# S5 phasor tables in half chunks with their own fragment, on a stream of their own in the first gate and up phase

## The chip, the core and the metric

The program runs on one core of a Trainium2 chip. TensorE (PE, with its weight loads PEld), VectorE (DVE), ScalarE (ACT) and GpSimd (POOL) each work through a list of instructions in order; SyncE (SP) holds the list of DMA issues, also in order. They wait for one another through semaphores. The metric is device time in microseconds of one launch.

## What is computed

Two layers of a streaming encoder on a sequence of 1024 positions and 1024 channels, float32. Layer 0 is forgetting attention followed by a SwiGLU; layer 1 is an S5 state-space mixer followed by another SwiGLU:

```python
def swiglu(h, w_gate, w_up, w_down):
    return (jax.nn.silu(h @ w_gate) * (h @ w_up)) @ w_down

def s5_mixer(h, w_in, log_dt, lam_re, lam_im, b_re, b_im, c_re, c_im, d_skip, w_glu, w_out):
    u = (h @ w_in).astype(f32)
    dt = jnp.exp(log_dt.astype(f32))[:, None]
    mag = jnp.exp(lam_re * dt)
    a_re = mag * jnp.cos(lam_im * dt)
    a_im = mag * jnp.sin(lam_im * dt)
    ...
    # x[k] = a * x[k-1] + (B u)[k] (complex, 64 groups of 64 states); y = Re(C x) + d * u
    y = jax.nn.gelu(y).astype(h.dtype)
    y = y * jax.nn.sigmoid(y @ w_glu)
    return y @ w_out
```

What S5 needs of its parameters alone (powers of `a`, products of these with `B` and `C`, and the phasors `e1 * e2`) does not depend on the data. The kernel makes these tables during the gate and up projections of layer 0, stores them in DRAM, and reads them back in the S5 mixer.

## The kernel before

**Gate and up.** `gate_up` (line 784) multiplies in 11 **pairs** p = 0..10 (one tile of gate with one of up, each with its partner half a matrix away). A pair is 14 **steps** s = 0..13 of 12 matmuls; each matmul is a product of high and low parts, and Strassen-like sums of weight quarters make 7 products do the work of 8. For each pair the weights are loaded as four 512 KB pages (`raw`, SP), summed on DVE (L819, L820, L825, L826), rounded to a high part on ACT (L807) and turned into a low part on DVE (L808). DVE and ACT also take the products out of PSUM (L871 to L888) and build the results `g_d` that SP stores (L898 to L906). The same function runs twice: in layer 0 (pairs from 762 to 1244 us of the trace) with the tables beside it, and in layer 1 (1810 to 2234 us) with nothing beside it.

**The tables beside it.** After the matmuls and the copies of a step, `gate_up` calls `next(beside)` if `when(p, s)` says so (L920). `beside` is the generator `s5_params` (L1129), and the set of steps is `(5, 9, 12)` in the pairs 2 to 9. After a start in pairs 0 to 2 it goes through 8 chunks, and each takes three calls:

1. *cp*: eight POOL products (L1183, L1184, L1187) into page `s5w0`, with `s5w1` as scratch. This is issued at step 12.
2. Step 5 of the next pair: the store of cp (L1197), 16 short matmuls on PE (L1201, **K matmuls**), two ACT copies and a POOL addition for `KT` (L1204, L1206, in `s5w1`), its store, then *bp*: six POOL products (L1237, L1238, L1239), again in `s5w0` with scratch `s5w1`.
3. Step 9: eight PE transposes of bp (L1168, **T transposes**), an ACT copy `T` into `s5w1` (L1170) and its store, then the **phasors** (`s5_rot`, L1217): six DVE products of 128x512 (L1237 to L1239, the helper `prod`), into `s5w0` with scratch `s5w1`. The phasors' store (L1228) is issued at the start of the next call, step 12, right ahead of the next chunk's cp.

So one chunk goes cp, K matmuls, KT, bp, T transposes, T, phasors and back to cp, always through the same two pages (28 and 32), each with one buffer: each stage waits until the stage before it has been read or stored.

**What sets the order.** The tile framework places the instructions of each engine in a fixed list when the kernel is built (nearly the program's order, with some moved by a priority), and adds the waits. `tc.issue_after(self.sp.ins)` keeps a store behind the latest weight load in SP's list. At run time every engine goes through its list in order.

**Names.** K matmuls and T transposes are also PE work: 16 and 8 short instructions for each chunk. `R1`, `R2`: the two factors of the phasors. `pw`: powers of `a`, read by cp and bp. `M`: a matrix of the mixer, whose first buffer lies in R1's page 30.

Of the kernel before, what the change touches and what calls it, by code (L numbers as in the profile page):

```python
# [20 lines left out]
NF = FF // P  # L21
# [137 lines left out]
class Trunk:  # L159
# [365 lines left out]
    def attend(self, c, o):  # L525
# [36 lines left out]
        def sums(hp):  # L562

            p2, r, x = self.pb(PTB, (P, P))[0:16], self.small("ri", (16, P)), self.R("RI")
            nc.tensor.transpose(p2, rs.pop(hp).rearrange("p a b -> p (a b)"), self.ident)
            nc.vector.reciprocal(r, p2)
            nc.sync.dma_start(self.ri_d[hp], r)
            for i in range(2):
                nc.sync.dma_start(x[i * 64:i * 64 + 64], self.bcast(self.ri_d[hp][i * 8:i * 8 + 8], D, 64))
            ri[hp] = x  # L570
# [213 lines left out]
    def gate_up(self, B, g_d, beside=iter(()), when=lambda p, s: False):  # L784

# [66 lines left out]
        for p in range(n):  # L852
# [11 lines left out]
            for s in range(14):  # L864
# [55 lines left out]
                if when(p, s):  # L920
                    next(beside, None)
# [82 lines left out]
    def s5_small(self):  # L1004
# [64 lines left out]
        pw = R("pw", (P, 2, 9, 32))  # L1069
# [59 lines left out]
    def s5_params(self):  # L1129
# [29 lines left out]
        self.T_d, self.rot_d, self.cp_d = (self.dram(n, [8, P, D]) for n in ("T_d", "rot_d", "cp_d"))  # L1159
# [14 lines left out]
        for ch in range(8):  # L1174
            if ch:
                finish(ch - 1, bp)
                yield from self.s5_rot(ch - 1)
# [37 lines left out]
        yield from self.s5_rot(7)  # L1215

    def s5_rot(self, ch):  # L1217

        R, sh, V = self.R, (P, 4, 8, 16), self.nc.vector
        pr = slice(4 * ch, 4 * ch + 4)  # L1220
        rot, k = R("s5w0", sh[:1] + (2,) + sh[1:]), R("s5w1", sh[:1] + (2,) + sh[1:])
        e1 = [self.R1[:, i, pr, None, :].to_broadcast(sh) for i in range(2)]
        e2 = [self.R2[:, i, pr, :, None].to_broadcast(sh) for i in range(2)]
        self.prod(V, rot[:, 0], e1[0], e2[0], e1[1], e2[1], ALU.subtract, k[:, 0])
        self.prod(V, rot[:, 1], e1[0], e2[1], e1[1], e2[0], ALU.add, k[:, 1])
        yield
        with self.tc.issue_after(self.sp.ins):
            self.nc.sync.dma_start(self.rot_d[ch], rot.rearrange("p i a b c -> p (i a b c)"))  # L1228
# [269 lines left out]
def trunk(ctx: ExitStack, tc: tile.TileContext, A, out):  # L1498
# [179 lines left out]
```

## Time and profile before

| | us |
|---|---|
| median of 3 runs | 2449.84 |
| lowest, highest | 2446.37, 2457.64 |
| the profiled execution, its own time | 2461.91 |
| its span, first to last instruction | 2460.0 |

| engine | busy us | share of the span |
|---|---|---|
| PE | 2371.6 | 96% |
| PEld | 1944.8 | 79% |
| DVE | 1745.1 | 71% |
| ACT | 1179.3 | 48% |
| POOL | 472.1 | 19% |

The profile describes one execution. Busy times are sums over an engine's instructions; "idle before, and what ended it" is put down to the semaphore that came last; the chain is followed back from the last instruction. A matmul's busy time overlaps the next, so a busy PE can still be slow. Times in the text are microseconds from the start of the span. Pairs are cut at the first matmul of each.

### The profile page before, as it was taken

How to read it: one execution, taken by the hardware profiler on the slowest of the kernel's cores; microseconds unless marked ns; L12 is line 12 of the kernel's file. 1: busy time of each engine (PE TensorE's matmuls, PEld its weight loads, DVE VectorE, ACT ScalarE, POOL GpSimd, SP SyncE). 2: the span in 40 equal slices, each digit the busy share in tenths (PEclk: the TensorE clock that was granted, in tenths of full speed). 3: DMA queues.
4: the chain of work that ended last, by engine and by line, in shares of the span. 5: the costliest groups of instructions: out<-in, count | busy, mean ns of one | idle time of the engine just before them, and what ended most of it. 6: DMA issues, size and time to landing. Idle time of an engine off the chain costs nothing.

```text
span 2460.0 us, 31616 instructions
## 1 busy us (share of the span) xinstructions
PE 2371.6 (96%) x11683; PEld 1944.8 (79%) x11683; DVE 1745.1 (71%) x2746; ACT 1179.3 (48%) x1997; POOL 472.1 (19%) x427
## 2 busy tenths in 40 slices
PE   7999999999999999999899999999999999999997
PEld 5787778777777887777678888988878888888886
DVE  6867776677678968687668676773686656555867
ACT  5767676667645343333344363332453333333344
POOL 3222222222300036456530001320000000000002
PEclk9999999999999999999999999999999999999999
DMA  4121111121344433334489752443333233237874
GB/s 126 60 66 52 49 47 61 54 59 52 101 149 108 124 105 133 123 121 139 152 293 320 225 185 77 133 142 123 117 99 129 88 118 111 91 116 253 288 233 154
DMA packets 252427, 318.23 MB, mean 129 GB/s; under 512 B 34225, under 2 KB 179937, under 8 KB 252273
## 3 DMA queue, kind: packets, MB, share of 16 engines
q1 hardware_dynamic: 252272, 316.23, 40.0%
q8 instruction: 91, 1.49, 0.3%
q14 instruction: 64, 0.52, 0.1%
HBM read 238.46 MB, written 77.72 MB: 129 GB/s over the span
## 4 chain that ended last, share of the span: by engine, by line
PE 67%; DVE 14%; ACT 7%; POOL 5%; issue 4%; DMA 3%; SPq 0%; DVEq 0%; POOLq 0%; ACTq 0%
PE ps L837 24%; PE ps L939 15%; PE ps L272 7%; PE ps L274 6%; PE ps L273 6%; PE ps L584 2%; PE ps L603 2%; DVE ps L551 2%; POOL s5w L1238 1%; DMA raw<-in_ffn_w_gate_dram 1%; POOL s5w L1239 1%; DVE p L434 1%; ACT wh L253 1%; ACT Pt L557 1%; POOL s5w L1187 1%
## 5 line engine op out<-in xcount | busy, mean ns | idle before, releaser
L837 PE MATMUL ps<-B,ah 128*128 128x512 f32 x1056 | 329.2, 393 | 0.3 <-ACT B L89 0.2
L939 PE MATMUL ps<-wdh,gl 128*128 128x512 f32 x616 | 241.4, 392 | 3.5 <-DVE gl L254 3.5
L939 PE MATMUL ps<-wdh,gh 128*128 128x512 f32 x616 | 241.4, 392 | 1.0 <-ACT gh L253 0.8
L939 PE MATMUL ps<-wdl,gh 128*128 128x512 f32 x616 | 241.1, 391 | 0.2 <-DVE wdl L254 0.2
L837 PEld LDWEIGHTS ps<-B,ah 128*128 128x128 f32 x1056 | 199.0, 189 | 42.6 <-ACT B L89 1.2
L837 PE MATMUL ps<-ops,ah 128*128 128x512 f32 x704 | 221.8, 396 | 5.0 <-ACT up L878 4.8
L272 PE MATMUL ps<-hT,wh 128*128 128x512 f32 x512 | 209.8, 410 | 9.2 <-DVE pt L409 7.3
L837 PE MATMUL ps<-B,al 128*128 128x512 f32 x528 | 206.7, 391 | 0.0
L273 PE MATMUL ps<-hT,wh 128*128 128x512 f32 x512 | 204.5, 399 | 0.0
L274 PE MATMUL ps<-hT,wl 128*128 128x512 f32 x512 | 202.3, 395 | 0.0
L253 ACT CAST gh<-gr 128x1024 fp32r<-128x1024 f32 (+1 forms) x78 | 81.1, 1040 | 202.7 <-PE ps L939 181.3
L588 DVE TENSOR_TENSOR ptl<-ps,pth 128x512 fp32r<-128x512 f32 x192 | 106.5, 555 | 85.5 <-ACT pth L587 80.8
L254 DVE TENSOR_TENSOR gl<-gr,gh 128x1024 fp32r<-128x1024 f32 (+1 forms) x78 | 98.3, 1262 | 88.8 <-ACT gh L253 88.8
L837 PEld LDWEIGHTS ps<-ops,ah 128*128 128x128 f32 x704 | 132.9, 190 | 35.5 <-ACT up L878 5.6
L1629 POOL TENSOR_TENSOR y<-m,s 128x512 f32<-128x512 f32 x4 | 6.6, 1642 | 764.7 <-DVE wdl L254 759.9
L543 POOL TENSOR_TENSOR An<-An,cmask 128x128 f32<-128x128 f32 x128 | 78.1, 612 | 370.7 <-DVE mx L551 342.5
L808 DVE TENSOR_TENSOR al<-raw,ah 128x1024 fp32r<-128x1024 f32 x88 | 112.9, 1287 | 45.5 <-ACT ah L807 45.3
L807 ACT CAST ah<-raw 128x1024 fp32r<-128x1024 f32 x88 | 92.4, 1050 | 108.2 <-PE ps L837 96.0
L939 PEld LDWEIGHTS ps<-wdh,gl 128*128 128x128 f32 x616 | 116.2, 189 | 28.9 <-DVE gl L254 5.0
L837 PE MATMUL ps<-ops,al 128*128 128x512 f32 x352 | 138.5, 394 | 0.0
L939 PEld LDWEIGHTS ps<-wdh,gh 128*128 128x128 f32 x616 | 116.4, 189 | 26.4 <-ACT gh L253 1.8
L939 PEld LDWEIGHTS ps<-wdl,gh 128*128 128x128 f32 x616 | 116.3, 189 | 24.8 <-DVE wdl L254 0.6
(353 smaller groups left out, 5927.9 us busy)
## 6 DMA issues: line engine op xcount, KB each, us to landing
raw<-in_ffn_w_down_dram SPq DMA_DIRECT2D x98, 512.0 KB, 5.3
gr<-g_d SPq DMA_DIRECT2D x76, 512.0 KB, 4.5
raw<-in_ffn_w_gate_dram SPq DMA_DIRECT2D x44, 512.0 KB, 4.0
raw<-in_ffn_w_up_dram SPq DMA_DIRECT2D x44, 512.0 KB, 4.1
g_d<-s SPq DMA_DIRECT2D x66, 256.0 KB, 2.1
raw<-in_fox_w_in_dram SPq DMA_DIRECT2D x32, 512.0 KB, 4.2
g_d<-up SPq DMA_DIRECT2D x22, 512.0 KB, 2.6
g_d<-up SPq DMA_DIRECT2D x44, 256.0 KB, 2.4
```

The costliest lines, as they stand in the source:

```text
L253: self.nc.scalar.copy(h, src)
L254: self.lsub.tensor_sub(l, src, f32(h))
L272: mm(ps, lh, rh, start=start, stop=False)
L273: mm(ps, lh, rl, start=False, stop=False)
L274: mm(ps, ll, rh, start=False, stop=stop)
L543: nc.gpsimd.tensor_add(An[h][:, qs], An[h][:, qs], self.cmask)
L551: nc.vector.tensor_tensor_reduce(out=ps[:, :nk], in0=ps[:, :nk], in1=An[h][:, :nk], op0=ALU.add, op1=ALU.min, scale=1.0, scalar=3e38, accu ...
L588: nc.vector.tensor_sub(dl, p2[:, 0:n], f32(dh))
L807: nc.scalar.copy(h, src)
L808: V.tensor_sub(l, src, f32(h))
L837: nc.tensor.matmul(bank, x[:, k], y, start=start and k == i == 0, stop=True, skip_group_check=True)
L939: nc.tensor.matmul(bank, x[:, j, t], y[:, j], start=start and i == 0, stop=True, skip_group_check=True)
```

## The change

The phasors leave `s5_params` and become a generator of their own. `s5_rot` now makes them in 16 half chunks of two columns (six DVE products of 128x256 instead of 128x512) into a tile `rot` of its own (one buffer of 2 KB a partition in pool `sq`), with scratch in 256 unused columns of the page of `pw`. Room comes from the tile `ri` of the attention, which has one buffer instead of four. `gate_up` calls a function `beside(p, s)` after each step: it advances the tables at steps 5 and 12 (no longer 9) of the pairs 3 to 10, and the phasors at steps 3 and 8 of the pairs from 2 on. A half chunk's store is issued at the next call of the phasors, behind the latest weight load, in 256 pieces of 1 KB.

A chunk of the tables then takes two calls: K matmuls, KT and bp at step 5; T transposes, T's store and the next chunk's cp at step 12. Pair 10 has chunk 7 at steps 5 and 12; before it had steps 5, 7, 9 and 11.

```diff
-            p2, r, x = self.pb(PTB, (P, P))[0:16], self.small("ri", (16, P)), self.R("RI")
+            p2, r, x = self.pb(PTB, (P, P))[0:16], self.sq.tile([16, P], F32, tag="ri", name=self.nm("ri")), self.R("RI")
...
-                if when(p, s):
-                    next(beside, None)
+                beside(p, s)
...
-        pw = R("pw", (P, 2, 9, 32))
+        pw = R("pw")
+        self.rk = pw[:, 576:832].rearrange("p (a b c) -> p a b c", a=2, b=8)
+        pw = pw[:, 0:576].rearrange("p (i n a) -> p i n a", i=2, n=9)
...
         for ch in range(8):
             if ch:
                 finish(ch - 1, bp)
-                yield from self.s5_rot(ch - 1)
             pr = slice(4 * ch, 4 * ch + 4)
...
         finish(7, bp)
-        yield from self.s5_rot(7)
-
-    def s5_rot(self, ch):
-
-        R, sh, V = self.R, (P, 4, 8, 16), self.nc.vector
-        pr = slice(4 * ch, 4 * ch + 4)
-        rot, k = R("s5w0", sh[:1] + (2,) + sh[1:]), R("s5w1", sh[:1] + (2,) + sh[1:])
...
-        self.prod(V, rot[:, 0], e1[0], e2[0], e1[1], e2[1], ALU.subtract, k[:, 0])
-        self.prod(V, rot[:, 1], e1[0], e2[1], e1[1], e2[0], ALU.add, k[:, 1])
-        yield
-        with self.tc.issue_after(self.sp.ins):
-            self.nc.sync.dma_start(self.rot_d[ch], rot.rearrange("p i a b c -> p (i a b c)"))
+
+    def s5_rot(self):
+
+        sh, V = (P, 2, 8, 16), self.nc.vector
+        self.rot_d = self.dram("rot_d", [8, P, D])
+        for j in range(16):
+            pr = slice(2 * j, 2 * j + 2)
+            rot = self.sq.tile([P, 2, 2, 8, 16], F32, tag="rot", name=self.nm("rot"))
...
+            self.prod(V, rot[:, 0], e1[0], e2[0], e1[1], e2[1], ALU.subtract, self.rk)
+            self.prod(V, rot[:, 1], e1[0], e2[1], e1[1], e2[0], ALU.add, self.rk)
+            yield
+            d = self.rot_d[j // 2].rearrange("p (i x n) -> p i x n", i=2, x=2)[:, :, j % 2]
+            with self.tc.issue_after(self.sp.ins):
+                self.nc.sync.dma_start(d, rot.rearrange("p i a b c -> p i (a b c)"))
...
-    first = {0: (8, 10, 12), 1: (5, 6, 8, 9, 10), NF // 2 - 1: (5, 7, 9, 11)}
+    params, rot, first = T.s5_params(), T.s5_rot(), {0: (8, 10, 12), 1: (5, 6, 8, 9, 10), 2: (5, 9, 12)}
+
+    def beside(p, s):
+        if s in first.get(p, (5, 12)):
+            next(params, None)
+        if p > 1 and s in (3, 8):
+            next(rot, None)
+
     B = Operands(T)
-    gu = T.gate_up(B, g_d[0], T.s5_params(), lambda p, s: s in first.get(p, (5, 9, 12)))
+    gu = T.gate_up(B, g_d[0], beside)
```

On PE the K matmuls stay behind step 5, and the T transposes move from behind step 9 to behind step 12 in the pairs 3 to 9 (in pair 10 from behind step 8). Line numbers of the changed kernel differ by one in `gate_up` (L836 for L837) and by one in `prod` (L1238 to L1240).

DVE, pair 7, around steps 9 to 11 of the kernel before (`s5w0` and `s5w1` are the two pages of the tables, `s`, `up` the results, `ps` PSUM, `al` low parts):

```order
L880 TENSOR_TENSOR up_946_9180<-up_946_9180,ps_73 128x512
L862 TENSOR_TENSOR s_944_9178<-s_944_9178,up_946_9180 128x512
L1237 TENSOR_TENSOR s5w0_966_9385<-R1_768_7400,R2_769_7401 128x512 x2
L883 TENSOR_TENSOR s_943_9177<-s_944_9178,ps_73 128x512
L808 TENSOR_TENSOR al_969_9408<-raw_961_9338,ah_968_9407 128x1024
L1238 TENSOR_TENSOR s5w1_967_9386<-R1_768_7400,R2_769_7401 128x512 x2
L1239 TENSOR_TENSOR s5w0_966_9385<-s5w0_966_9385,s5w1_967_9386 128x512
L883 TENSOR_TENSOR up_945_9179<-up_946_9180,ps_73 128x512
L1239 TENSOR_TENSOR s5w0_966_9385<-s5w0_966_9385,s5w1_967_9386 128x512
L862 TENSOR_TENSOR s_943_9177<-s_943_9177,up_945_9179 128x512
```

DVE, pair 7 of the changed kernel, between the results of steps 3 and 8 (`rot285`, `rot286` are two half chunks of phasors, `pw` here their scratch):

```order
L861 TENSOR_TENSOR s_935_9220<-s_935_9220,up_937_9222 128x512
L1239 TENSOR_TENSOR pw_767_7399<-R1_768_7400,R2_769_7401 128x256
L818 TENSOR_TENSOR S_969_9579<-raw_954_9391 128x512
L1240 TENSOR_TENSOR rot285_9412<-rot285_9412,pw_767_7399 128x256
L1239 TENSOR_TENSOR pw_767_7399<-R1_768_7400,R2_769_7401 128x256
L819 TENSOR_TENSOR S_959_9470<-S_959_9470,raw_945_9315 128x512
L1238 TENSOR_TENSOR rot286_9607<-R1_768_7400,R2_769_7401 128x256 x2
L1240 TENSOR_TENSOR rot286_9607<-rot286_9607,pw_767_7399 128x256
L1239 TENSOR_TENSOR pw_767_7399<-R1_768_7400,R2_769_7401 128x256
L1240 TENSOR_TENSOR rot286_9607<-rot286_9607,pw_767_7399 128x256
L1239 TENSOR_TENSOR pw_767_7399<-R1_768_7400,R2_769_7401 128x256
L807 TENSOR_TENSOR al_951_9370<-raw_923_9074,ah_950_9369 128x1024
```

The phasors moved from the end of the pair to its first half, around the wait for the first `raw` page of the next pair (L819, L820 before), and `rot286` begins behind the store of `rot285`.

SP, from step 9 of pair 7 to step 5 of pair 8 of the kernel before (`g0` to `g3` are the stored results):

```order
L899 DMA g01_d_92<-s_944_9178 128x512
L1171 DMA T_d_7907<-s5w1_965_9382 128x1024
L1228 DMA rot_d_7908<-s5w0_966_9385 128x1024
L900 DMA g02_d_93<-up_945_9179 128x1024
L904 DMA g00_d_91<-s_944_9178 128x512
L905 DMA g01_d_92<-up_946_9180 128x512
L906 DMA g03_d_94<-up_946_9180 128x512
L231 DMA raw_986_9574<-in_ffn_w_gate_dram 128x8x128
L1197 DMA cp_d_7909<-s5w0_973_9451 128x1024
L231 DMA raw_994_9648<-in_ffn_w_up_dram 128x8x128
```

SP at the same place of the changed kernel:

```order
L899 DMA g02_d_93<-up_937_9222 128x1024
L1171 DMA T_d_7923<-s5w1_962_9498 128x1024
L903 DMA g00_d_91<-s_936_9221 128x512
L904 DMA g01_d_92<-up_938_9223 128x512
L905 DMA g03_d_94<-up_938_9223 128x512
L231 DMA raw_976_9632<-in_ffn_w_gate_dram 128x8x128
L231 DMA raw_984_9706<-in_ffn_w_up_dram 128x8x128
L1229 DMA rot_d_7726<-rot286_9607 256x1x256
L1196 DMA cp_d_7924<-s5w0_963_9501 128x1024
L231 DMA raw_975_9630<-in_ffn_w_gate_dram 128x8x128
```

T's store now stands behind the store of the summed result `g2`, and both loads of the second `raw` pages stand ahead of cp's store instead of on either side of it.

POOL, end of cp in pair 8 and bp in pair 9 of the kernel before:

```order
L1187 TENSOR_TENSOR s5w0_1005_9759<-s5w1_1006_9760 64x4x128 x2
L1237 TENSOR_TENSOR s5w0_1020_9911<-bb_782_7584,pw_767_7399 128x512 x2
L1206 TENSOR_TENSOR s5w1_1019_9906<-s5w1_1019_9906,R2_769_7401 16x8x16
L1238 TENSOR_TENSOR s5w1_1021_9912<-bb_782_7584,pw_767_7399 128x512 x2
L1239 TENSOR_TENSOR s5w0_1020_9911<-s5w0_1020_9911,s5w1_1021_9912 128x512 x2
```

The same of the changed kernel:

```order
L1186 TENSOR_TENSOR s5w0_993_9816<-s5w1_994_9817 64x4x128 x2
L1254 MEMSET M_1372_12271 128x1024
L1238 TENSOR_TENSOR s5w0_1008_9976<-bb_782_7584,pw_767_7399 128x512 x2
L1205 TENSOR_TENSOR s5w1_1007_9971<-s5w1_1007_9971,R2_769_7401 16x8x16
L1239 TENSOR_TENSOR s5w1_1009_9977<-bb_782_7584,pw_767_7399 128x512 x2
L1240 TENSOR_TENSOR s5w0_1008_9976<-s5w0_1008_9976,s5w1_1009_9977 128x512 x2
```

The clearing of `M` came from pair 10 into pair 9, ahead of bp; it waits for the last phasors, and the eight small loads of `M` from `KT_d` stand in SP's list of pair 9 (before, they were spread over the down projection).

## Rows read from the trace of the kernel before

**Rows 1.** Stretches: us, busy (x instructions) by engine, PEclk, DMA share, GB/s.

```profile
847.47:887.37 39.90, 39.90 (x185) 33.22 (x184) 30.74 (x53) 15.48 (x22) 10.22 (x7) 1.00 0.31 99
887.37:1244.29 356.92, 334.07 (x1537) 268.84 (x1536) 276.51 (x284) 130.53 (x200) 190.32 (x126) 0.98 0.42 139
972.68:1021.00 48.32, 44.13 (x193) 35.11 (x192) 34.63 (x36) 16.20 (x25) 26.70 (x18) 0.93 0.34 116
1063.51:1105.87 42.36, 40.71 (x193) 32.92 (x192) 35.59 (x37) 16.08 (x25) 23.91 (x17) 1.00 0.40 133
1148.46:1196.38 47.92, 42.43 (x193) 34.21 (x192) 35.02 (x36) 16.20 (x25) 27.10 (x18) 0.96 0.36 118
1196.38:1244.29 47.91, 43.64 (x193) 34.90 (x192) 32.38 (x33) 17.70 (x25) 25.78 (x19) 0.93 0.65 214
1891.51:1929.59 38.08, 38.08 (x169) 31.55 (x168) 22.49 (x31) 14.00 (x19) 0.00 (x0) 1.00 0.37 118
```

**Rows 2.** Waits, 847 to 1245 us: who for whom, total us, times, longest.

```profile
POOL s5w L1183 <- DVE s5w L1239: 61.4, 7, 9.8
PE ps L1168 <- POOL s5w L1239: 14.4, 10, 4.0
PE ps L837 <- ACT up L878: 4.8, 2, 2.5
PE ps L837 <- DVE al L808: 3.3, 4, 1.4
```

**Rows 3.** Timeline of POOL, pair 7: start, us, what [idle before <-releaser].

```profile
1081.92 2.39 POOL L1237 TENSOR_TENSOR s5w<-bb,pw 128x512 f32<-128x512 f32 x2 [7.82 <-PE ps L1201]
...
1086.80 3.91 POOL L1238 TENSOR_TENSOR s5w<-bb,pw 128x512 f32<-128x512 f32 x2 [2.08 <-DMA KT_d<-s5w]
1090.67 3.41 POOL L1239 TENSOR_TENSOR s5w<-s5w,s5w 128x512 f32<-128x512 f32 x2
...
1103.13 1.44 POOL L1183 TENSOR_TENSOR s5w<-cc,pw 128x512 f32<-128x512 f32 x1 [8.19 <-DVE s5w L1239]
...
1113.13 3.33 POOL L1187 TENSOR_TENSOR s5w<-s5w 64x512 f32<-64x512 f32 x2
```

**Rows 4.** Timeline of PE, pair 3: the K matmuls.

```profile
904.15 1.05 PE L1201 MATMUL ps<-s5w,R 128*16 128x128 f32 x16
```

**Rows 5.** Timeline of SP and POOL: one store in pair 7, cp's first product in pair 4.

```profile
1066.54 0.32 SPq L900 DMA_DIRECT2D g_d<-up  x1
...
969.94 4.39 POOL L1183 TENSOR_TENSOR s5w<-cc,pw 128x512 f32<-128x512 f32 x1 [8.18 <-DVE s5w L1239]
```

**Rows 6.** Line L1237: x count, duration ns min/median/max, first and last start.

```profile
L1237 POOL TENSOR_TENSOR s5w<-bb,pw x16: 1094/1106/2088, 905.4 to 1217.7; 128x512 f32<-128x512 f32 x16
L1237 DVE TENSOR_TENSOR s5w<-R,R x16: 684/685/692, 920.1 to 1228.1; 128x512 f32<-128x512 f32 x16
```

**Rows 7.** Timeline of DVE: a product of 128 columns; one op beside POOL, and alone.

```profile
841.01 0.38 DVE L1124 TENSOR_TENSOR R<-s5t 128x128 f32<-128x128 f32 x1
...
1061.16 2.14 DVE L808 TENSOR_TENSOR al<-S,ah 128x1024 fp32r<-128x1024 f32 x1
...
1963.68 1.22 DVE L808 TENSOR_TENSOR al<-S,ah 128x1024 fp32r<-128x1024 f32 x1
```

**Rows 8.** DMA issues, 847 to 1245 us: x count, KB each, median us to landing.

```profile
g_d<-s SPq DMA_DIRECT2D x27, 256.0 KB, 2.1
T_d<-s5w SPq DMA_DIRECT2D x8, 512.0 KB, 2.9
rot_d<-s5w SPq DMA_DIRECT2D x8, 512.0 KB, 3.0
```

**Rows 9.** Timeline of ACT: the copy of T in pair 7.

```profile
1095.30 1.01 ACT L1170 COPY s5w<-ps 128x1024 f32<-128x1024 f32 x1 [1.08 <-PE ps L1168]
```

**Rows 10.** Timeline of PE: pair 10's T transposes; the first wait of the down projection.

```profile
1224.64 0.47 PE L1168 MATMUL ps<-ident,s5w 128*128 128x128 f32 x1 [4.04 <-POOL s5w L1239]
...
1252.35 0.50 PE L939 MATMUL ps<-wdh,gl 128*128 128x512 f32 x1 [1.49 <-DVE gl L254]
```

More of the change, by code (lines that the diff above doesn't have):

```diff
@@ L782, in ffn_plan, with gate_up @@
             self.plan((src, (P, src.shape[1], 512), op, None, None))
-    def gate_up(self, B, g_d, beside=iter(()), when=lambda p, s: False):
+    def gate_up(self, B, g_d, beside=lambda p, s: None):
         nc, R = self.nc, self.R
@@ L1158, in s5_params @@
         yield
-        self.T_d, self.rot_d, self.cp_d = (self.dram(n, [8, P, D]) for n in ("T_d", "rot_d", "cp_d"))
+        self.T_d, self.cp_d = (self.dram(n, [8, P, D]) for n in ("T_d", "cp_d"))
         self.KT_d = self.dram("KT_d", [8, 16, D])
@@ L1214, in s5_params @@
         finish(7, bp)
-        yield from self.s5_rot(7)
-    def s5_rot(self, ch):
-        R, sh, V = self.R, (P, 4, 8, 16), self.nc.vector
-        pr = slice(4 * ch, 4 * ch + 4)
-        rot, k = R("s5w0", sh[:1] + (2,) + sh[1:]), R("s5w1", sh[:1] + (2,) + sh[1:])
-        e1 = [self.R1[:, i, pr, None, :].to_broadcast(sh) for i in range(2)]
-        e2 = [self.R2[:, i, pr, :, None].to_broadcast(sh) for i in range(2)]
-        self.prod(V, rot[:, 0], e1[0], e2[0], e1[1], e2[1], ALU.subtract, k[:, 0])
-        self.prod(V, rot[:, 1], e1[0], e2[1], e1[1], e2[0], ALU.add, k[:, 1])
-        yield
-        with self.tc.issue_after(self.sp.ins):
-            self.nc.sync.dma_start(self.rot_d[ch], rot.rearrange("p i a b c -> p (i a b c)"))
+    def s5_rot(self):
[4 more added lines that the diff above has]
+            rot = self.sq.tile([P, 2, 2, 8, 16], F32, tag="rot", name=self.nm("rot"))
+            e1 = [self.R1[:, i, pr, None, :].to_broadcast(sh) for i in range(2)]
+            e2 = [self.R2[:, i, pr, :, None].to_broadcast(sh) for i in range(2)]
+            self.prod(V, rot[:, 0], e1[0], e2[0], e1[1], e2[1], ALU.subtract, self.rk)
[4 more added lines that the diff above has]
+                self.nc.sync.dma_start(d, rot.rearrange("p i a b c -> p i (a b c)"))
     def pwr(self, i, o, pr):
```

## The prediction, on record before the run

> **What bounds the kernel now.** I first read the shares of the engines: PE is busy for 2371.6 of 2460.0 us, so only what stops PE or slows its stream counts. Next came stretches of whole pairs [rows 1]. The row to start from is the last: a pair of layer 1, which runs the same 168 matmuls with nothing beside it, takes 38.08 us (169 instructions). Pair 2 of layer 0, with 16 short instructions more, takes 39.90 us. The eight pairs 3 to 10, with 16 K matmuls and 8 T transposes each, take 356.92 us, a mean of 44.6 us. Pair 7 takes 42.36; pairs 5, 9 and 10 take 48 each and show a granted clock of 0.93 to 0.96, where the others show 1.00. So there is time to be had in pairs 3 to 10, if these waits can go.
>
> Whom does PE wait for? The waits of this stretch [rows 2] name T transposes waiting for bp (14.4 us in 10 waits), results waiting for ACT (4.8 in 2) and for a low part of DVE (3.3 in 4). The largest wait is not PE's: POOL waits 61.4 us in 7 waits before cp, for the last phasor product. Pair 7 on POOL shows the chain [rows 3]: bp starts at 1081.92, waits 2.08 us for KT's store and ends at 1094.1, which is 12.2 us; cp can start only at 1103.13, 8.19 us after POOL's last work, and ends at 1116.46, 13.3 us later. From step 5 to step 9 PE has 4 steps of 38.08/14 = 2.72 us, so 10.9 us: bp is late by 1.3 us in an ordinary pair. In pair 10 the same wait is 4.04 us [rows 10].
>
> The long pairs have a cause behind cp. In pair 4 its first product took 4.39 us [rows 5], where another took 1.44 [rows 3]; DVE was working without a gap beside it. Such a cp is stored late, its store stands in SP's list ahead of the second load of `raw`, so this page and with it the sums and low parts of pair 5 are late. That the clock then falls to 0.93 follows the stops, as far as these rows show: no pair without them has it.
>
> **The change, part by part.** *bp.* The T transposes go from step 9 to step 12: bp has 7 steps, 19.0 us, for its 12.2 us. The wait of 1.3 us in each pair, and the 4.04 us of pair 10, go. Next behind is the T copy and what follows it.
>
> *From T to cp.* The path that is now tight runs from step 12 to step 5 of the next pair, again 7 steps or 19.0 us. T copy 1.01 us [rows 9], T's store 2.9 us to landing [rows 8], cp 13.3 us [rows 3]: 17.2 us. The slack is 1.8 us. Before, cp had the phasors and their store ahead of it. What this path newly holds is the place of T's store in SP's list: behind the store of `g2`, which waits for DVE's last results. If those are on time it costs nothing; the first rival takes the other case.
>
> *The phasors on DVE.* Twelve products of 128x256 for six of 128x512. A product of 512 columns was recorded at 0.685 us [rows 6], one of 128 columns at 0.38 [rows 7]; the line between puts 256 columns at 0.48. So 12 products are 5.8 us of DVE in a pair for 4.1 before, 1.7 us more. That is the upper bound, since the recorded ends of such products reach into the next one; the lower is no more at all, the columns being the same. DVE is busy for 35.59 us of pair 7's 42.36, so it has 6.8 us free; the new place, behind steps 3 and 8, is about where DVE waits for the next `raw` page. I cost it at nothing on the path; if that cover is gone, the 5.8 us come ahead of a low part, and PE stops for what they exceed its lead.
>
> *One buffer for `rot`.* The second half chunk waits for the first one's store. A store of 256 KB lands in 2.1 us and one of 512 KB in 3.0 [rows 8]. It is issued in the call at step 8, so DVE stands for at most about 2 us there, with the low part for step 9 on behind it. I estimate slack of 2 us there, and price it at 0 to 1 us a pair.
>
> *PE.* The number of short instructions is the same. 16 short transposes made pair 2 longer by 1.82 us, so 8 cost 0.91; the K matmuls cost 1.05 [rows 4] to 1.1. A pair without a wait is then 38.08 + 0.91 + 1.1 = 40.1 us.
>
> *Pair 2, `M`, `ri`.* The first phasors come into pair 2, ahead of a sum for step 5: I take 0.8 us for it, between 0 and the 2.9 us of one half chunk. The clearing of `M` stands ahead of bp in one pair: about 1 us (one POOL product is 1.106 [rows 6]), inside bp's new slack. `ri` with one buffer lies in the attention, where its uses are a whole head pair apart: nothing.
>
> *Sum.* Eight pairs of 40.1 are 320.7; 356.92 − 320.7 = 36.2 us less. I do not think that all waits go: those of ACT and of low parts have other causes, and their sizes (4.8/2 and 3.3/4 us) suggest 0.5 us a pair, 4.0 us in all (0 to 10). So −36.2 + 0.8 + 4.0 = −31.4 us. On the profiled execution that is 2461.91 − 31.4 = 2430.5.
>
> That execution is 12.07 us above the median, about the spread of the three runs (11.27 us). If the difference is spread over everything, the median becomes 2418.4. If the median run simply lacked the extra of pairs 5 and 9 (48.32 + 47.92 − 2 × 42.5 = 11.2 us), only 20.2 us are left to gain: 2429.6. I take the middle, **2424 us**.
>
> The row on which the price of the phasors hangs is one and the same form on DVE, the low part of 128x1024: 2.14 us beside POOL and 1.22 alone [rows 7]; it waited for a whole product of POOL, about 1 us. The Trainium skill, "SBUF — State Buffer", section "Who interferes with whom", says that a DVE instruction with two SBUF inputs contends with a GpSimd instruction that reads SBUF, and that whoever issues first holds the shared pair for its whole length. That speaks against this change, which doubles the number of such DVE instructions and puts them beside cp and bp. By it the sum would be the second rival's; the trace agrees that DVE waits, with the 0.92 us above, but not that each of the 16 products of POOL stops it.
>
> **The rivals.** *T's store is late (0.18).* In pair 7 the issue of `g2`'s store stood at 1066.54 [rows 5], 3.0 us into pair 7, for results of pair 6. If DVE is as late as that in the changed kernel, T's store behind it lands 5.9 us into the pair and cp ends at 19.2, where the K matmuls stand at 6 × 2.72 = 16.3: 2.9 us of stop in each of eight pairs, 23.2 us, and 8 us of gain are left: 2442, or 2453 where the median has no long pairs. For it: DVE is busiest exactly at the pair's end. Against it: the phasors have gone from there, which is 4.1 us of DVE ahead of the last results. Within 0.5%.
>
> *The shared port (slower, 0.08).* DVE is busy for 22.49 us of the free pair and 35.59 of pair 7 [rows 1]; 4.1 of the 13.1 are phasors, so 9.0 us are waiting inside instructions, beside some 16 POOL products. If each of the 16 stopped DVE for its 1.1 us, that is 17.6, and DVE would need 22.5 + 5.8 + 17.6 = 45.9 us, with 2 of its 6.8 idle us left 48 in a pair. It decides from the point where DVE's need passes the old mean of 44.6. Then 8 × 3.4 = 27 us more: 2477. For it: twice as many small instructions, and POOL without its 8 us pause before cp, which lets more of its work meet DVE's. Against it: POOL's number of products stays, and the 9.0 us are about half of the most that is possible.
>
> *Given back at the down projection (0.10).* Pair 10's DMA share is 0.65 [rows 1]; in 40.1 us the same transfers are 0.78, and its first matmuls waited already, 1.49 us once [rows 10]. If the 7.8 us by which pair 10 is shorter are waited there, the time is 2432.
>
> *It does not do what it says (0.04).* `rot`'s store could land so late (8 us for the 2.1 of the row) that DVE holds the low parts of step 9: 3 to 5 us a pair, so 2448 to 2464: no change on the whole.
>
> **How the numbers follow.** Forecast 0.60 (its own range 2411 to 2437), late store 0.18, port 0.08, given back 0.10, `rot` 0.04. A measurement of this kernel tells about 0.5%, 12.2 us, from no change: faster is below 2437.6, slower above 2462.1. Faster: 0.60 + 0.10 and a little of the late store, 0.72. Same: 0.19. Slower: 0.09. The low end, 2411, has no residual waits (−4.0), the whole difference spread, and the down projection's own 1.5 us gained, with some 2 us for runs. The high end, 2444, takes in the given-back case and two thirds of the late store; 0.06 + 0.08 + 0.04 = 0.18 is left above it, and 0.02 below.
>
> **What would show it.** Right: pairs 3 to 10 near 40.1 us each, granted clock 1.00 in pairs 5, 9 and 10; POOL starts cp 1 to 2 us into a pair instead of 8 us late, and its wait on phasors is gone from the waits; no T transpose waits for bp; low parts on DVE are not later than before. Wrong: K matmuls of step 5 wait for cp, by the late store (SP's issue of T's store more than 3 us into the pair) or by a cp of 15 us and more; results or low parts at step 9 wait for DVE, with L808's form at 2 us in most rows (port), or behind a `rot` product that waits for a DMA; a longer first step of the down projection than the one with the 1.49 us.

## The result, and the profile after

| | before | changed |
|---|---|---|
| median of 7 runs, us | 2454.31 | 2466.02 |
| lowest, highest | 2446.37, 2467.31 | 2464.28, 2472.93 |
| the profiled execution, us | 2461.91 | 2464.28 |

The changed kernel is a little slower: ratio 1.0043, 95% interval 1.0022 to 1.0064, inside the 0.5% that I had called no change and clear of 1. I had forecast 2424 us, with a range of 2411 to 2444. The sign was wrong, and the time lies 22 us above the range; 4.5 us of that come from the reference, since the kernel before has a median of 2454.31 here where I had started from 2449.84.

Stretches of the changed kernel, columns as in [rows 1]: pair 2, pairs 3, 4, 5, 7, 8, 9 and 10, and pairs 3 to 10 together.

```profile
848.83:889.70 40.87, 40.41 (x186) 33.05 (x184) 36.36 (x70) 15.24 (x22) 10.18 (x7) 1.00 0.34 110
889.70:939.84 50.14, 43.59 (x194) 34.91 (x192) 38.24 (x48) 15.98 (x25) 11.85 (x10) 0.93 0.33 108
939.84:987.57 47.73, 43.36 (x194) 35.06 (x193) 36.01 (x42) 16.23 (x25) 19.92 (x16) 0.93 0.37 118
987.57:1032.19 44.62, 42.09 (x193) 34.08 (x192) 34.90 (x42) 16.14 (x25) 20.15 (x16) 0.96 0.38 125
1077.03:1121.65 44.62, 42.08 (x194) 34.10 (x193) 34.39 (x42) 16.14 (x25) 20.15 (x16) 0.96 0.39 125
1121.65:1169.34 47.69, 42.50 (x194) 34.45 (x192) 36.77 (x42) 16.12 (x25) 19.91 (x16) 0.93 0.37 118
1169.34:1209.52 40.18, 40.18 (x194) 33.03 (x192) 30.08 (x35) 16.25 (x25) 22.18 (x17) 1.00 0.47 143
1209.52:1249.87 40.35, 40.35 (x193) 33.16 (x192) 21.34 (x22) 18.93 (x26) 26.04 (x19) 1.00 0.71 243
889.70:1249.87 360.17, 336.28 (x1537) 272.90 (x1536) 266.35 (x315) 132.01 (x201) 161.77 (x126) 0.96 0.42 136
```

Pairs 9 and 10 are what I had expected of all eight, 40.2 and 40.4 us at a granted clock of 1.00. Pair 10 was 47.91 in [rows 1]. Pairs 3 to 8, where two half chunks of phasors lie in each, take 44.6 to 50.1 us. Pair 9 has only one half chunk on DVE (35 of DVE's instructions instead of 42).

The waits of this stretch (who for whom, total, times, longest) answer to [rows 2].

```profile
PE ps L836 <- DVE al L807: 24.3, 8, 5.7
DVE rot L1238 <- DMA rot_d<-rot: 6.9, 8, 1.4
POOL s5w L1182 <- DMA T_d<-s5w: 110.0, 6, 20.6
```

PE's waits for bp (14.4 us) and ACT (4.8) are gone, and so are POOL's 61.4 us of waiting for the phasors. In their place PE waits for low parts of DVE: 24.3 us in 8 waits, where it was 3.3. They fall mostly on step 9, which lasts 6.6 to 10.8 us in pairs 3 to 8 and 2.72 in pair 9.

DVE in pair 7 of the changed kernel, around step 9 (start, us, what, idle before it), and POOL in the same pair:

```profile
1094.45 0.41 DVE L1240 TENSOR_TENSOR rot<-rot,pw 128x256 f32<-128x256 f32 x1
1094.90 1.23 DVE L1239 TENSOR_TENSOR pw<-R,R 128x256 f32<-128x256 f32 x1
1097.27 0.77 DVE L819 TENSOR_TENSOR S<-S,raw 128x512 f32<-128x512 f32 x1 [1.15 <-DMA raw<-in_ffn_w_gate_dram]
1098.55 0.76 DVE L1238 TENSOR_TENSOR rot<-R,R 128x256 f32<-128x256 f32 x2 [0.50 <-DMA rot_d<-rot]
1099.23 0.42 DVE L1240 TENSOR_TENSOR rot<-rot,pw 128x256 f32<-128x256 f32 x1
1099.68 1.26 DVE L1239 TENSOR_TENSOR pw<-R,R 128x256 f32<-128x256 f32 x1
1100.97 1.21 DVE L1240 TENSOR_TENSOR rot<-rot,pw 128x256 f32<-128x256 f32 x1
1102.22 1.40 DVE L1239 TENSOR_TENSOR pw<-R,R 128x256 f32<-128x256 f32 x1
1103.54 3.67 DVE L807 TENSOR_TENSOR al<-raw,ah 128x1024 fp32r<-128x1024 f32 x2
```

```profile
1079.51 1.10 POOL L1182 TENSOR_TENSOR s5w<-cc,pw 128x512 f32<-128x512 f32 x1 [15.82 <-DMA T_d<-s5w]
...
1094.67 2.41 POOL L1238 TENSOR_TENSOR s5w<-bb,pw 128x512 f32<-128x512 f32 x2 [4.03 <-PE ps L1200]
...
1099.55 2.35 POOL L1239 TENSOR_TENSOR s5w<-bb,pw 128x512 f32<-128x512 f32 x2 [2.06 <-DMA KT_d<-s5w]
1101.86 2.88 POOL L1240 TENSOR_TENSOR s5w<-s5w,s5w 128x512 f32<-128x512 f32 x2
```

This is the loss of pair 7 in one picture. The second half chunk stands ahead of the low part (L807) that step 9 needs. Its first product waits 0.50 us for the store of the first half chunk. A product takes 0.41 us as long as POOL waits for KT's store, and 1.2 to 1.4 us from 1099.55 on, when bp's next products run. The low part begins at 1103.54, when PE has been waiting for it since 1103.2, and is itself stretched to 2.29 us beside bp's last products (1.22 alone); PE goes on at 1105.87. Step 9 on PE: the matmul that waited, then stretches with the columns of [rows 1], the wait itself, the rest of step 9, and step 10.

```profile
1105.87 0.50 PE L836 MATMUL ps<-ops,al 128*128 128x512 f32 x1 [2.54 <-DVE al L807]
```

```profile
1102.71:1105.87 3.16, 0.62 (x3) 0.19 (x1) 3.16 (x3) 0.00 (x0) 3.16 (x3) 1.00 0.00 0
1105.87:1109.84 3.97, 3.97 (x10) 3.13 (x11) 3.31 (x5) 0.63 (x1) 0.25 (x1) 0.57 0.45 132
1109.84:1112.58 2.74, 2.74 (x13) 2.25 (x12) 1.90 (x3) 0.00 (x0) 0.00 (x0) 1.00 0.00 0
```

The stop has a tail. The ten matmuls behind it take 3.97 us at a granted clock of 0.57, where ten at full clock take ten twelfths of a step of 2.72 us, 2.27: 1.7 us more. Then the clock is back at 1.00. The 24.3 us of waiting thus cost more than their own length.

The chain of waits of pair 7 says it in order (start, us, what):

```profile
1094.89 3.63 DMA rot_d<-rot
...
1103.54 2.29 DVE al L807
```

Two causes are in it: the products that are stretched beside POOL (call it **port**), and the one buffer of `rot`, with the landing of a store between two half chunks (**buffer**). A third one was possible: in SP's list the store of cp, which waits for POOL, stands ahead of a load of `raw` (**queue**).

### The profile page after: what moved, and what is told of

It reads as the page before. It is cut to its first block, busy times and chain, and to the rows that moved or that the text cites. A ratio compares the mean times of both kernels' runs of the same rounds, so it can differ in the third digit from the quotient of the medians.

```text
span 2462.5 us, 31641 instructions
## 1 busy us (share of the span) xinstructions
PE 2370.9 (96%) x11683; PEld 1945.8 (79%) x11683; DVE 1739.0 (71%) x2794; ACT 1179.5 (48%) x1997; POOL 445.7 (18%) x427
## 4 chain that ended last, share of the span: by engine, by line
PE 68%; DVE 17%; ACT 7%; issue 4%; DMA 3%; POOL 0%; SPq 0%; DVEq 0%; ACTq 0%; POOLq 0%
PE ps L836 27%; PE ps L937 14%; PE ps L272 6%; PE ps L273 6%; PE ps L274 6%; PE ps L584 2%; PE ps L603 2%; DVE ps L551 2%; DVE al L807 2%; DMA rot_d<-rot 1%; ACT wh L253 1%; DVE p L434 1%; DVE rot L1240 1%; ACT Pt L557 1%; DMA raw<-in_ffn_w_gate_dram 1%
## 5 line engine op out<-in xcount | busy, mean ns | idle before, releaser
L836 PE MATMUL ps<-B,ah 128*128 128x512 f32 x1056 | 328.4, 392 | 0.3 <-ACT B L89 0.2
L836 PEld LDWEIGHTS ps<-B,ah 128*128 128x128 f32 x1056 | 200.2, 190 | 43.6 <-ACT B L89 1.2
L836 PE MATMUL ps<-ops,ah 128*128 128x512 f32 x704 | 225.2, 402 | 0.0
L836 PE MATMUL ps<-B,al 128*128 128x512 f32 x528 | 206.2, 390 | 0.0
L836 PE MATMUL ps<-ops,al 128*128 128x512 f32 x352 | 142.6, 405 | 23.1 <-DVE al L807 23.1
L254 DVE TENSOR_TENSOR gl<-gr,gh 128x1024 fp32r<-128x1024 f32 (+1 forms) x78 | 97.0, 1245 | 92.6 <-ACT gh L253 91.4
L836 PEld LDWEIGHTS ps<-ops,ah 128*128 128x128 f32 x704 | 135.5, 194 | 29.9 <-issue 1.7
L807 DVE TENSOR_TENSOR al<-raw,ah 128x1024 fp32r<-128x1024 f32 x88 | 115.2, 1317 | 46.1 <-ACT ah L806 45.9
```

The lines of the kernel that those rows point to most:

```text
L254: self.lsub.tensor_sub(l, src, f32(h))
L807: V.tensor_sub(l, src, f32(h))
L836: nc.tensor.matmul(bank, x[:, k], y, start=start and k == i == 0, stop=True, skip_group_check=True)
```

## The experiments

In the order of what they tell apart. The sum over pairs 3 to 8 is the measure; without any wait it is 6 x 40.18 = 241.08 us, and it is 279.64 in the changed kernel, an excess of 38.6 us: the waits and their tails. The runs were taken on three chips, each beside the kernel before; the changed kernel itself was not timed on them again. So they are compared with it by the stretches of one profiled execution each, and with the kernel before by the ratios at the end of this section.

### The kernel before, again

> The kernel before, unchanged, for a second profile of it. If the long pairs 5 and 9 of the first profile are an accident of one execution, their 48 us come at other pairs or not at all, and the time is 2447 to 2454 us; if they belong to the kernel they stand at the same pairs again.

2450.12 us (median, 10 runs). In this profile pairs 5 and 9 are ordinary, pair 10 is as long as before:

```profile
972.39:1014.93 42.54, 40.76 (x193) 32.92 (x192) 35.77 (x37) 16.07 (x25) 24.04 (x17) 1.00 0.39 132
1142.81:1185.60 42.79, 40.92 (x193) 32.91 (x192) 35.91 (x37) 16.07 (x25) 24.11 (x17) 1.00 0.39 132
1185.60:1233.52 47.92, 43.54 (x193) 35.04 (x192) 32.90 (x33) 17.74 (x25) 25.90 (x19) 0.93 0.64 216
887.46:1233.52 346.06, 329.39 (x1537) 265.43 (x1536) 278.39 (x284) 130.25 (x200) 185.48 (x126) 0.99 0.43 144
```

So the 48 us of pairs 5 and 9 in [rows 1] do not belong to every execution; those of pair 10 are in both. Against this execution there were 346.06 − 8 × 40.18 = 24.6 us to be had, not 36. Pairs 3 to 8 sum to 255.35 here: the change makes them 24.3 us longer, and pairs 9 and 10 (90.7 us here, 80.5 after) 10.2 us shorter.

### Without the phasors

```diff
-            rot = self.sq.tile([P, 2, 2, 8, 16], F32, tag="rot", name=self.nm("rot"))
+            if not j:
+                rot = self.sq.tile([P, 2, 2, 8, 16], F32, tag="rot", name=self.nm("rot"))
...
+            if not j:
                 self.prod(V, rot[:, 0], ...)
                 self.prod(V, rot[:, 1], ...)
```

> Leaves out the phasor products of all half chunks but the first; the 16 stores stay and send the first half chunk each time. Theory port (the twelve products of a pair are stretched beside POOL's cp and bp, and stand ahead of the low part that step 9 needs) and theory buffer (DVE waits for the store of the half chunk before): both expect pairs 3 to 8 at 40.1 to 40.5 us instead of 44.6 to 50.1, about 38 us less on the whole, near 2428 us. Theory queue (the store of cp stands ahead of a load of raw in SP's list and makes it late) expects pairs 3 to 8 to stay at 43 us or more, 2455 us or more.

2428.45 us; pairs 3 to 8 sum to 242.36, and step 9 has 2.72 us in each. All of the loss hangs on the phasors' products on DVE. The queue theory falls: POOL, cp's store and its place in SP's list were the same. The trace of the changed kernel agrees: in pair 7 the load of `raw` behind cp's store (1090.66) is issued at 1093.02, right behind the low part of 1091.78 (1.21 us), not behind the store.

### POOL's products replaced by clearings

```diff
-                G.tensor_tensor(kg[:, 0], self.coef(self.cc, i, pr), self.pwr(0, 0, pr), op=ALU.mult)
+                G.memset(kg[:, 0], 0.0)
...
-            self.prod(G, bp[:, 0], ...)
-            self.prod(G, bp[:, 1], ...)
+            for i in range(2):
+                G.memset(bp[:, i], 0.0)
+                G.memset(k[:, i], 0.0)
+                G.memset(bp[:, i], 0.0)
```

> POOL's products of cp and bp are replaced by as many clearings of the same tiles, so that POOL writes and does not read there; its contents are then zeros. DVE's phasors, their store and the order of the lists stay. Theory port: the six products of a half chunk take 2.0 to 2.7 us from first to last instead of 5 to 6, the low part of step 9 is on time, and pairs 3 to 8 come to 40.1 to 41 us, 2430 us on the whole. Theory buffer: the wait of 0.5 to 1.4 us for the store and the 3.6 us of its landing stay, and pairs 3 to 8 stay over 43 us.

2426.3 us; every pair from 3 to 10 takes 40.18. DVE's second half chunk in pair 7 (start, us, what):

```profile
1067.67 1.03 DVE L1238 TENSOR_TENSOR rot<-R,R 128x256 f32<-128x256 f32 x2 [0.59 <-DMA rot_d<-rot]
1068.62 0.41 DVE L1240 TENSOR_TENSOR rot<-rot,pw 128x256 f32<-128x256 f32 x1
1069.07 0.43 DVE L1239 TENSOR_TENSOR pw<-R,R 128x256 f32<-128x256 f32 x1
...
1070.33 1.22 DVE L807 TENSOR_TENSOR al<-raw,ah 128x1024 fp32r<-128x1024 f32 x1
```

The wait for the store is still there (0.59 us), and it costs nothing, because the six products take 2.7 us instead of 5.0. POOL's products are needed for the loss. A clearing takes 0.53 us where a product takes 1.1, so the length differs too; but beside clearings DVE is not stretched at all. The low part of 1070.33 takes 1.22 us, as alone, while POOL clears:

```profile
1070.45 0.99 POOL L1210 MEMSET s5w<- 128x512 f32 x2 [1.58 <-DMA KT_d<-s5w]
```

Of the phasors' products in this trace (pairs 3 to 9), 14 met a clearing and nothing else, and they took 0.41 to 0.43 us. What stretches DVE is thus something that a product does and a clearing doesn't (both write, the product also reads), and not the length of POOL's work.

### The buffer's wait, first attempt

```diff
-                self.nc.sync.dma_start(d, rot.rearrange("p i a b c -> p i (a b c)"))
+                self.nc.sync.dma_start(d, self.R1[:, :, 0:16].rearrange("p i a b -> p i (a b)"))
```

> The 16 stores read a part of R1's page instead of the half chunk's tile (so wrong values are stored), and the next half chunk need not wait for them; their number, size and place in SP's list stay. Theory buffer: the stop at step 9 falls from 4.2 us and more to under 1 us in pairs 3 to 8, near 2435 us. Theory port: only the 6.9 us that DVE waited for the stores in eight places go, at most 0.9 us a pair, so pairs 5 to 7 at 43.5 to 44.5 us and 2459 us or more.

2445.74 us, between both expectations, and the run doesn't test what it was made for. With no store to wait for, the framework's planner put the phasors as early as it could: the last half chunk is begun by 949.7, and pair 3 has 94 instructions on DVE:

```profile
889.79:945.70 55.91, 46.93 (x193) 36.73 (x192) 54.84 (x94) 18.33 (x29) 10.88 (x10) 0.88 0.28 91
1066.57:1106.75 40.18, 40.18 (x193) 33.03 (x192) 28.00 (x30) 16.11 (x25) 22.05 (x16) 1.00 0.45 140
```

What it shows is the price of half chunks in a heap: pair 3, with nine of the 16, takes 55.9 us, and pairs 5 to 8, without phasors, 40.2 (pairs 9 and 10 take 41.1 and 40.6).

### The buffer's wait, with the order held

The same, and each half chunk behind an instruction of DVE that stands ahead of it in the changed kernel's list too.

```diff
+            with self.tc.issue_after(self.pins[j % 2].ins):
                 self.prod(V, rot[:, 0], ...)
                 self.prod(V, rot[:, 1], ...)
...
-                self.nc.sync.dma_start(d, rot.rearrange("p i a b c -> p i (a b c)"))
+                self.nc.sync.dma_start(d, self.R1[:, :, 0:16].rearrange("p i a b -> p i (a b)"))
```

> As in the run before it, the stores read R1's page and not the half chunk's tile, so wrong values are stored and no half chunk waits for a store; but now each half chunk is held at the place that it has in the changed kernel's list of DVE (behind the low part of the sums S1, S2, and behind the difference that waits for raw). Theory port: the wait of 0.5 to 1.4 us goes and the six products still take 4 to 5 us beside bp, so pairs 5 to 7 at 43 to 44.5 us, 2452 to 2462 us in all. Theory buffer: pairs 5 to 7 at 40.2 to 41 us, under 2440 us.

2445.1 us: both numbers were wrong. Pairs 3 to 8 sum to 260.30, an excess of 19.2 instead of 38.6 us. Two of its stretches, pairs 4 and 7, and two of DVE's products in pair 7:

```profile
931.54:976.04 44.50, 41.80 (x194) 33.93 (x192) 36.32 (x44) 16.24 (x25) 21.70 (x16) 0.96 0.42 134
1060.28:1105.75 45.47, 41.80 (x193) 33.93 (x192) 36.67 (x44) 16.26 (x25) 20.50 (x16) 0.96 0.42 131
```

```profile
1084.02 1.33 DVE L1243 TENSOR_TENSOR rot<-rot,pw 128x256 f32<-128x256 f32 x1
...
1086.63 1.37 DVE L1243 TENSOR_TENSOR rot<-rot,pw 128x256 f32<-128x256 f32 x1
```

Half of the excess goes with the wait for the store; half stays, with no store to wait for and products still stretched beside bp. In pairs 3 to 10 PE waits 13.1 us for low parts instead of 23.9, so 10.8 us less for a wait of 6.3 us there, and the tails shrink from about 15 to 6 us (excess less waits). The half that stays is the port's alone. The half that goes is not spread evenly: pair 3 goes from 50.1 to 41.7 us, but pair 7 gains nothing (45.5 us for 44.6), so its stop is the port's alone. Where the wait did count, it needed POOL's products beside it: without them the same wait cost nothing.

### Phasors on POOL, behind bp

```diff
-        sh, V = (P, 2, 8, 16), self.nc.vector
+        sh, V = (P, 2, 8, 16), self.nc.gpsimd
...
+            with self.tc.issue_after(self.pin.ins) if self.pin else nullcontext():
                 self.prod(V, rot[:, 0], ...)
...
-        if p > 1 and s in (3, 8):
+        if p > 1 and s in (6, 10):
```

(`pin` is bp's last product.)

> The whole computation, with the twelve products of a pair on POOL instead of DVE, behind bp in its list, where POOL waits 12 us for T's store. Theory port: DVE has nothing more ahead of the low part of step 9, so the stop at step 9 goes (2.7 us a step); POOL takes about 7 us for the products, and its reading stretches DVE's last results by up to 0.6 us each; pairs 4 to 10 at 40.2 to 41 us, 2428 to 2436 us. If POOL is the limit (cp starts late), the K matmuls wait at step 5 instead and pairs stay over 42 us.

2447.85 us. Step 9 has 2.72 us in pairs 3 to 10, as expected. The twelve products took 14.2 us in pair 7, not 7 (1084.46 to 1098.70): 0.61 us each where DVE doesn't stop them, 1.07 where it does, and a wait for the store. T's store, behind DVE's last results (1.0 to 1.2 us each beside POOL instead of 0.69), is issued 2 us into the pair; so cp came late, and the K matmuls waited at step 5 (8.7 us in 6 waits); pairs 3 to 9 take 40.9 to 42.1 us. Pair 10 takes 51.8, by the late store again: in SP's list T's store stands behind a store of phasors, which waits for POOL until 1182, and six loads of `M`. It is issued 10.7 us into the pair, and cp begins at 1191.55, 14.4 us into it.

```profile
1174.30 8.23 SPq L1231 DMA_DIRECT2D rot_d<-rot  x2
...
1187.88 0.38 SPq L1171 DMA_DIRECT2D T_d<-s5w  x1
```

### Phasors on DVE at the end of the pair

```diff
-        if p > 1 and s in (3, 8):
+        if p > 1 and s in (0, 2, 10, 11):
```

(One call for the products, one for the store. The first half chunk stands behind the low part made in step 10, the second behind the last result.)

> The whole computation, phasors on DVE, held at the end of the pair (behind the low part made in step 10) and at the start of the next one, when POOL has no product in hand. Theory port: six products take 2 us at each place; step 9 is free. The 2 us stand ahead of the last results and so ahead of g2's store and T's store behind it: if cp starts 2 us later than the 2.4 to 4.4 us of the changed kernel, the K matmuls wait up to 2 us at step 5: pairs 4 to 9 at 40.2 to 42.2 us, 2430 to 2446 us.

2440.0 us. A product takes 0.41 to 0.42 us at the pair's end, where POOL waits, and step 9 is free (2.72 us in pairs 4 to 10). Pairs 5 to 9 take 42.0 to 42.2 (pair 4 takes 43.6, over the range): step 5 has 5.5 to 5.8 us instead of 3.8, and PE waits 10.0 us in 7 waits for cp. The number lies in the range, but not for the reason expected. T's store isn't late: in pairs 5 to 9 it is issued 0.9 to 1.0 us ahead of the pair, and cp starts 3.0 to 4.7 us into it, much as in the changed kernel. It is cp that is longer, 13.4 to 15.1 us instead of 11 to 12: phasors at the pair's start run beside it. Its first product in pair 7, which starts at 1055.83, takes 2.81 us instead of 1.10, beside products of DVE at 0.42:

```profile
1059.35 2.81 POOL L1182 TENSOR_TENSOR s5w<-cc,pw 128x512 f32<-128x512 f32 x1 [12.41 <-ACT s L870]
```

So this is the port again, with POOL as the one that waits.

### Phasors on DVE in its two gaps

```diff
-        if p > 1 and s in (3, 8):
+        if p > 1 and s in (0, 3, 8):
...
+            with self.tc.issue_after(self.pin.ins) if self.pin else nullcontext():
                 self.prod(V, rot[:, 0], ...)
...
             bp, k = ...
+            G.memset(self.rk[:, 0, 0, 0:1], 0.0)
```

(`pin` is the latest low part or, at a pair's start, the last result. The clearing ahead of bp waits for the second half chunk.)

> The whole computation, phasors on DVE, held in its list at two places: the first half chunk at the start of a pair, ahead of the 5 us that DVE waits for raw; the second behind the low part for step 8, ahead of DVE's second wait for raw, and bp on POOL begins only when it is done (a clearing of one column of the scratch stands ahead of bp). The store of the first has 10 us. Theory port: the second half chunk takes 2 to 2.7 us instead of 5, the low part of step 9 is on time, bp ends within its 19 us: pairs 4 to 10 at 40.2 to 40.8 us, 2426 to 2434 us. If position or the number of instructions and not POOL's reading was the cause, step 9 waits as before and the pairs stay at 43 us and more.

2427.15 us, ratio to the kernel before 0.991 (0.9893 to 0.9926). Pairs 3 to 8 sum to 243.18; a half chunk takes 2.3 us from first to last in both places.

> As dve_gaps, without the clearing that holds bp back: the second half chunk stands behind the low part for step 8 and ahead of DVE's wait for raw, while bp may run beside it. If POOL's reading is what costs, its six products take 4 to 5 us where bp has begun (2.3 us in dve_gaps), but DVE waited another 2.6 us for raw behind them there, so the pairs lose at most 0.5 us each: 40.2 to 40.9 us, 2426 to 2436 us. If the hold was needed, the pairs go back over 42 us.

The same without the clearing: 2426.82 us, ratio 0.9852 (0.9834 to 0.987), on a chip on which the kernel before took 2461.56. Every pair from 3 to 9 takes 40.18 us. The stretch of pairs 3 to 10, and DVE's second half chunk in pair 7:

```profile
889.98:1211.54 321.56, 321.56 (x1538) 264.30 (x1537) 264.35 (x321) 132.69 (x201) 172.20 (x126) 1.00 0.47 152
```

```profile
1067.22 0.41 DVE L1241 TENSOR_TENSOR rot<-R,R 128x256 f32<-128x256 f32 x1
...
1068.67 0.42 DVE L1242 TENSOR_TENSOR pw<-R,R 128x256 f32<-128x256 f32 x1
1069.13 1.35 DVE L1243 TENSOR_TENSOR rot<-rot,pw 128x256 f32<-128x256 f32 x1
1071.82 0.69 DVE L819 TENSOR_TENSOR S<-S,raw 128x512 f32<-128x512 f32 x1 [1.35 <-DMA raw<-in_ffn_w_gate_dram]
```

POOL's products are those of the changed kernel in form and number, and so are DVE's; five of these six products meet none of POOL's, the sixth, from 1069.13 on, meets bp's first and takes 1.35 us. Two of the first half chunk's meet cp and take 1.2 to 1.3 us, ahead of a wait for `raw` of 2 us, so that they cost nothing. The 1.35 us of waiting for `raw` behind it are what is left of the cover. So the place of the products alone decides, and the clearing wasn't needed. This version beats both kernels, by their ratios to the kernel before (0.985 here, 1.004 for the changed kernel).

### The second half chunk behind the low part of step 9

```diff
-        if p > 1 and s in (3, 8):
+        if p > 1 and s in (0, 3, 6, 8):
```

(First half chunk as in the gaps; the second behind the low part that step 9 needs, without a wait for a store.)

> The whole computation; first half chunk at the start of the pair as in dve_gaps, the second behind the low part for step 9 instead of ahead of it, in the middle of bp, with no wait for a store. If the stop at step 9 comes from what stands ahead of that low part, step 9 has 2.72 us in every pair. The port theory expects the six products to take 5 us and more there (up to six products of POOL in a row, 1.2 to 1.4 us each), so that the results of steps 8 to 11 come late: PE then waits at a later step, up to 2 us a pair, 2430 to 2444 us; without stretching nothing waits and the time is 2426 to 2430.

2441.76 us. Step 9 has 2.72 us in pairs 4 to 10: the stop there did come from what stood ahead of its low part. The stop came back at the next pair's step 5 (5.3 to 6.5 us for 3.8). In pair 7, which starts at 1057.87, DVE's products, and SP and POOL at its start:

```profile
1084.35 1.34 DVE L1241 TENSOR_TENSOR pw<-R,R 128x256 f32<-128x256 f32 x1
...
1088.40 1.40 DVE L1241 TENSOR_TENSOR pw<-R,R 128x256 f32<-128x256 f32 x1
```

```profile
1059.79 0.34 SPq L899 DMA_DIRECT2D g_d<-up  x1
1060.22 0.38 SPq L1171 DMA_DIRECT2D T_d<-s5w  x1
```

```profile
1064.82 1.18 POOL L1182 TENSOR_TENSOR s5w<-cc,pw 128x512 f32<-128x512 f32 x1 [17.34 <-DMA T_d<-s5w]
```

DVE loses about 4 us of each pair to the stretched products. Its last results and the store of `g2` come 1.9 us into the next pair, T's store behind it at 2.4, and cp begins at 7.0, where 3.4 was early enough in the run before. It is the first rival's chain, set off by the second rival's cause.

The ratios to the kernel before on the same chip, with their 95% intervals (the kernel before had medians of 2449.97 us on chip 4, 2448.82 on chip 6 and 2461.56 on chip 9):

| run | chip | ratio |
|---|---|---|
| the kernel before, again | 4 | 0.9993 (0.9977 to 1.0008) |
| without the phasors | 4 | 0.9903 (0.9876 to 0.993) |
| clearings on POOL | 4 | 0.9894 (0.9869 to 0.9918) |
| the buffer's wait, first attempt | 4 | 0.9981 (0.9969 to 0.9993) |
| the buffer's wait, order held | 6 | 0.9987 (0.9977 to 0.9997) |
| phasors on POOL | 6 | 0.9997 (0.9985 to 1.0008) |
| phasors at the end of the pair | 6 | 0.9962 (0.995 to 0.9975) |
| phasors in the gaps, with the clearing | 6 | 0.991 (0.9893 to 0.9926) |
| phasors in the gaps, without it | 9 | 0.9852 (0.9834 to 0.987) |
| second half chunk behind step 9 | 9 | 0.9907 (0.9884 to 0.993) |

## Why the prediction was wrong

**What bounds the kernel now: right.** bp and the phasors on one path bounded pairs 3 to 10, and without a wait a pair takes 40.18 us (I had worked out 40.1). T transposes wait for nothing any more, and pair 10 went from 47.91 to 40.35 us. Pair 2 grew by 0.97 us; I had put 0.8. The clearing of `M` held bp for 3.4 us without a stop.

**The size of what was to be had: too large.** The sum was made against an execution with two long pairs. I named that as one of two readings and took the middle; the second profile of the kernel before lacks them and leaves 24.6 us. The two gap versions came to 2427.2 and 2426.8 us, close to the 2424 of the forecast, though not by this change: 21.7 us under the kernel before on one chip and 34.7 on another, where the kernel before took 2461.56, as long as the first profile's execution. How often the long pairs come, two profiles don't show.

**The step that failed: "The phasors on DVE", priced at nothing on the path.** I counted 5.8 us for twelve products, by durations from places where POOL was idle: the row of [rows 6] stands in a stretch where POOL waits for these very products, and the row of 128 columns in [rows 7] before the first cp. In the new place a product takes 0.41 us beside an idle POOL and 1.2 to 1.5 beside a busy one, so 5.0 us for the second half chunk of pair 7 alone, and 9.4 to 12.6 us for the twelve of a pair (10.4 in pair 7; pairs 3 to 8). The row that held the right price was in the same group: a low part of 2.14 us beside POOL and 1.22 alone, 0.92 us for one instruction. I applied it to the rival and not to the sum. Twelve times 0.92 is 11 us more, against 6.8 us that DVE had free. Measured, it was 5.4 us more in pair 7 than twelve products of 0.42: 40 of the 77 products of pairs 3 to 9 were stretched, not all.

**The cover that failed.** I let the wait for `raw` hide the products and wrote that a low part would pay if the cover was gone. The second half chunk doesn't stand ahead of that wait but behind it (L819 comes first in the list), and right ahead of the low part of step 9. The rows of the order that stand in the section on the change show just that; I read the place by the number of the call (step 8), not by its neighbours.

**One buffer for `rot`: the mechanism right, its size wrong.** The wait is 0.5 to 1.4 us, near my 0 to 1, behind a store that landed in up to 6.7 us where I had the 2.1 us of [rows 8]. But with the stretched products there was no slack left for it, and freeing it takes half of the excess away.

**From T to cp: right, with two errors that cancel.** T's store landed in 4.9 us (median), not 2.9, so that cp starts 2.5 to 4.5 us into a pair; cp took 11 to 12 us instead of 13.3 and ends 13.6 to 16.0 us into pairs 4 to 9, ahead of the K matmuls at 16.4 (step 5 has 3.8 us). I had put the slack at 1.8 us. The late store, my first rival, did not happen here; it did in two of the versions above (phasors on POOL, and behind step 9).

**The rivals.** The slower rival named the cause, DVE and POOL at one port, and ended at 2477 us; I gave it 0.08. Its point of decision (DVE's need over 44.6 us a pair) was wrong: DVE is busy for 34.4 us of pair 7, less than before. It is not the sum of DVE's work in a pair that decides but the 5 us that stand ahead of one low part. The rival on `rot` (0.04, 2448 to 2464) had that place right. Nothing was given back at the down projection: from its start to that of layer 1's pairs it took 565.5 us before and 564.6 after.

The Trainium skill's rule ("SBUF — State Buffer", section "Who interferes with whom": a DVE instruction with two SBUF inputs contends with a GpSimd instruction that reads SBUF, for the whole instruction) agrees with these traces: 0.41 us alone, 0.43 beside clearings, 1.2 to 1.5 beside products. I had said that the trace didn't show that each POOL product stops DVE; beside bp nearly each did, one for one, as DVE had a run of short instructions there.

What stays open: why the freed buffer took 10.8 us of PE's waits away for 6.3 us of its own, and why in some pairs and not in pair 7 (the store may also have kept the list behind it late). No run has products of 128x512 in the new place, so what the halving alone cost isn't shown.

## What to carry to other kernels

An instruction's price is that of its new neighbours: when work is moved off a chain, look for what the chain kept apart. Here the wait that the change removed (POOL waiting for DVE's phasors) was also what kept the two engines from meeting. Read from the order which instruction stands right behind moved work and who waits for it, and pin work that has no inputs to wait for (`issue_after`), since a planner puts it wherever the engine looks free.

## What the runs showed of the hardware

Short DVE products beside a run of POOL products alternate with them, one for one: 128x256 takes 0.41 us alone and 1.2 to 1.5 us there. A low part of 128x1024 loses about as much (2.29 us for 1.22), so that, by these rows, halving the size doubles the number of waits and not the work. Beside clearings, which only write, neither loses anything. It holds the other way too: a POOL product of 128x256 took 0.61 us where DVE didn't stop it, and up to 1.19 us beside busy DVE; cp's first product, of 128x512, took 2.81 us beside a run of DVE's products (phasors at the end of the pair) and 1.10 without them.

A stop of PE of some 2.7 us was followed by ten matmuls at a granted clock of 0.57 (of 2.4 GHz, so near the lower of its two levels, 1.2), 1.7 us more than at full clock. In the version with phasors at the end of the pair, with stops of up to 1.8 us, pairs 3 to 8 show 1.00, and so does the version without stops, through 321.56 us on end.
